# A hybrid decoder step: x turned before the launch, norms applied after the projections, decode selection first, and weight chunks of eight slices

## The chip, the cores and the metric

The kernel runs on one core of a Trainium2 chip. Its engines run side by side, each on its own queue in a fixed order: TensorE (PE: matmuls, transposes), VectorE (DVE), ScalarE (ACT), GpSimd (POOL) and SyncE (SP, which issues the DMA transfers here). The metric is the device time of one execution in microseconds. Three executions of the kernel before took 2206.09, 2209.12 and 2209.97 us; the median is 2209.12.

## The reference

One layer over 1024 prompt tokens and 32 decode tokens (8 sequences of 4), model width 2048. All inputs and weights are fp32.

```
xn = rmsnorm(x, norm_in)                       # mean square over 2048, times norm_in
p  = xn @ w_in    # q 8x128, k 2x128, v 2x128, z_attn 1024, q_idx 16x64, k_idx 64, w_idx 16,
                  # h, b, c, z_conv 1024 each
q, k, k_idx: rmsnorm over a head, then rotary on a quarter
I[t,s] = sum_h w_idx[t,h] * relu(q_idx[t,h] . k_idx[s])     # admissible s <= t
idx = top_k(I, 256)                            # prompt: of 1024; decode: of 8192 cached + own
attn = softmax(q . k[idx]) @ v[idx]            # decode gathers the selected rows from paged caches
conv, new_buf = width-3 causal convolution of c * h
mix = concat[attn * silu(z_attn), b * conv * silu(z_conv)]
y = x + mix @ w_out;   also returned: k, v, k_idx per token, conv buffers
```

## The kernel before

The tokens are worked in two blocks. Block 0 is prompt tokens 0 to 511 and the 32 decode tokens, 544 columns in two PSUM halves: 288 (prompt 256 to 511 and decode) and 256. Block 1 is prompt tokens 512 to 1023, 512 columns. In each block the same stages follow: index queries (`qi_tiles`, 8 tiles of 128 weight columns; in block 0 on the half of 288 alone), index keys (`ki_tile`, 80 weight columns), heads (`head_tiles`: 2 k, 2 v, 8 q), 8 gates (`z_tile`), and 8 convolution tiles (`conv_tiles`: c, h, b, z_conv). In block 0 the order is index queries, then index keys; in block 1 keys, then queries. Then come the output projections (`out_proj0` for block 0, `out_proj1` for block 1).

Every projection (`proj`) is exact to fp32 in three products: x and w are split into a rounded part and a remainder (xh, xl; wh, wl), and xh*wh, xl*wh and xh*wl are summed over 16 slices of 128 along the model width (L512). `load_w` loads a chunk of four such slices (tile w, 4 buffers), ScalarE casts it to wh and VectorE subtracts for wl (3 buffers each). A matmul of a slice so needs a chunk's wh and wl and the slice's xh and xl.

x comes in rows of tokens. `prep_x0` loads the rows of block 0, takes their norms (`x_rstd`), scales the rows, and then transposes them on TensorE (psx) slice by slice; `x_part` writes xh (ScalarE) and xl (VectorE) from PSUM, times norm_in. Block 1: `x_rms1` takes the norms on the side, `x1_load` loads the rows (xq), `x1_scale` scales them by rx1, and `prep_x1` transposes them between the matmuls of the last convolution tile of block 0 (`conv_tiles(0, 7)`).

The rest is side work in four pipes that are advanced at every `slot()` between chunks: main (scores of the index, attention), dec (decode attention), rms, and vec (the selections). A prompt selection (`prompt_select`) searches a threshold for the scores of 128 tokens; a prompt attention (`prompt_attend`) makes probabilities P, transposes them (pt) and multiplies with v. The decode selection (`decode_find`) compacts the selected positions of 32 tokens in a tile S of 128x2304 int16 in several rounds (L1226 to L1237: each round has two tensor_scalar and three tensor_tensor instructions on VectorE), takes the maximum over ways (`way`, L1239), and makes row numbers (`pg`, `nb`, `pt`, `ids`, `pidx`, `rid`) for the gathers. "dsel" is its end, and the heads of block 1 wait for it.

What order the engines' queues get is settled before the launch by the framework's list scheduler, which follows the program order and priorities (`first()` raises one); on the chip each engine takes its queue strictly in that order. VectorE's helper instructions all carry the line L121.

Of the kernel before, what the change touches and what calls it, by code (L numbers as in the profile page):

```python
# [8 lines left out]
F32 = mybir.dt.float32  # L9
# [104 lines left out]
def build(tc, ctx, I, O, stop=None):  # L114
# [80 lines left out]
    def w_in(ch, c0, m):  # L195

        if c0 == C_KI:
            return I["w_ki"][:, 4 * ch:4 * ch + 4]
        return I["w_in"][c0 // 128 if c0 < C_KI else 28 + (c0 - C_H) // 128, :, 4 * ch:4 * ch + 4]

    def w_out0(ch, c0, m):
        return I["w_out0"][c0 // 128, :, 4 * ch:4 * ch + 4]

    x_src = [(0, 128, xpr[256:384]), (256, 32, xsa), (128, 128, xpr[384:512]),
             (288, 128, xpr[0:128]), (416, 128, xpr[128:256])]
    x_raw = []

    def x_load(j):

        c0, n, src = x_src[j]  # L210
        if j == 0:
            big = gp.tile([128, 2304], F32, tag="sc", bufs=1, name="xsc")
            nc.sync.dma_start(big[:, 0:D], src)
            x_raw.append((c0, n, [(1024 * h, 1024, big[:, 1024 * h:1024 * h + 1024]) for h in range(2)]))
            return
        elif j < 4:
            parts = [(1024 * h, 1024, g4(name="xs")) for h in range(2)]
        else:
            parts = [(512 * h, 512, g2(name="xs2")) for h in range(4)]
        for a, w, t in parts:  # L220
            nc.sync.dma_start(t[:n, :w], src[:, a:a + w])
        x_raw.append((c0, n, parts))

    ident = const((128, 128), "ident")
    rows = e2((128, 256), name="rows")
    x_load(0)
    x_load(1)
    x_load(2)
    nc.vector.memset(rows, 0.0)
    nc.sync.dma_start(ident, I["cst"][:, 0:128])  # L230
    nc.sync.dma_start(rows[0:16, 0:128], I["norm_in"].rearrange("o (c p) -> (o c) p", p=128))
    nc.sync.dma_start(rows[32:56, 0:128], I["w_conv"].rearrange("o j (c p) -> (o j c) p", p=128))
    nc.sync.dma_start(rows[:, 128:256], I["state_conv"].rearrange("o s j (c p) -> (o s j c) p", p=128))
# [42 lines left out]
    w_d = dp.tile([512], F32, name="w_d", tag="w_d")  # L276

# [57 lines left out]
    rx1 = const((128, 4), "rx1")  # L335

    def x_part(k, ps, xs, hi, lo, a, w):

        for c0, n, parts in xs:
            if a <= c0 < a + w:  # L340
                for a2, w2, t in parts:
                    if a2 <= 128 * k < a2 + w2:
# [7 lines left out]
    def x_rstd(js, eng="av"):  # L350

        n = len(js)
        ss = sm((128, 2, n, 2), name="ssx")
        nc.vector.memset(ss, 0.0)
        for c, j in enumerate(js):
            _, rows_, parts = x_raw[j]
            for h, (a, w, t) in enumerate(parts):
                sqx = e2((128, 1024), BF, name="sqx")
                o = ss[:rows_, h % 2, c, h // 2:h // 2 + 1]
                if eng[h % 2] == "a":  # L360
                    nc.scalar.activation(out=sqx[:rows_, :w], in_=t[:rows_, :w], func=AF.Square, accum_out=o)
                else:
                    nc.vector.tensor_tensor_reduce(out=sqx[:rows_, :w], in0=t[:rows_, :w], in1=t[:rows_, :w], scale=1.0,
                                                   scalar=0.0, op0=MUL, op1=ADD, accum_out=o)
        v = sm((128, n), name="vx")
        tt(ss[:, 0], ss[:, 0], ss[:, 1], ADD)
        tt(v, ss[:, 0, :, 0], ss[:, 0, :, 1], ADD)
        ts(v, v, 1.0 / D, EPS, MUL, ADD)
        return rsqrt(v, n, "rx")

    def x_scale(j, h, r, c, eng=None):
        _, n, parts = x_raw[j]
        a, w, t = parts[h]
        if eng is nc.scalar:
            nc.scalar.activation(out=t[:n, :w], in_=t[:n, :w], func=AF.Copy, scale=r[:n, c:c + 1])
        else:
            (eng.tensor_scalar if eng else ts)(t[:n, :w], t[:n, :w], r[:n, c:c + 1], None, MUL)

    def prep_x0():

        x = x_tiles()

        def second():
            yield 1
            yield 1
            x_load(3)
            x_load(4)
            yield 1
            yield 1
            r = x_rstd((3, 4))  # L390
            for _ in range(4):
                yield 1
            for c, j in enumerate((3, 4)):
                for h in range(len(x_raw[j][2])):
                    x_scale(j, h, r, c)
            for _ in range(2):
                yield 1
            for k in range(KT):
                x_part(k, pj(name="psx"), x_raw, *x[k], 288, 256)
                yield 1  # L400
            hp[0] = 200
# [1217 lines left out]
```

## Time and profile before

| | |
|---|---|
| median of three runs | 2209.12 us |
| profiled execution | 2209.53 us, of which the span is 2207.6 us |
| TensorE | 2162.5 us busy, 98% of the span |
| VectorE, ScalarE, GpSimd | 1317.3, 1088.3 and 480.5 us |
| mean granted TensorE clock | 0.995 |
| DMA | 290.81 MB, mean 132 GB/s |

TensorE is busy nearly all the time, so a reader looks for the places where it is not, and for what ended each wait. The page's granted clock is 1.00 for 2.4 GHz; 0.50 is 1.2 GHz.

### The profile page before, as it was taken

The page shows a single profiled execution, that of the slowest core. Times are in us where ns is not written, and L with a number is a line of the kernel's source. Part 1 is how long each engine was busy: PE and PEld are TensorE (multiplying, and loading weights), DVE is VectorE, ACT ScalarE, POOL GpSimd, SP SyncE. Part 2 cuts the span into 40 slices and gives each one's busy share as a digit, 9 for nine tenths or more (in the row PEclk, how much of TensorE's full clock was granted, in tenths as well). Part 3 has the DMA queues.
Part 4 walks back from the last instruction along what each step waited for, and adds up shares of the span by engine and source line. Part 5 has one row for each costly group of instructions (what it writes and reads, how often), then busy time and mean ns, then how long its engine had stood idle before and what let it go on. Part 6 is the DMA issues. An engine that isn't in the chain of part 4 may idle for free.

```text
span 2207.6 us, 37829 instructions
## 1 busy us (share of the span) xinstructions
PE 2162.5 (98%) x13502; PEld 1941.8 (88%) x13502; DVE 1317.3 (60%) x2994; ACT 1088.3 (49%) x2112; POOL 480.5 (22%) x697
## 2 busy tenths in 40 slices
PE   6999999999999999999899999999999999999999
PEld 5899999999999999787688888888888899999887
DVE  6556666555555654799866666556667556443222
ACT  4346666334436566422257684445675565332221
POOL 2111011111113222142531143432331111210000
PEclk9999999999999999999999999999999999999999
DMA  5423444344344333333343344433343384448343
GB/s 195 131 90 117 125 138 135 118 141 131 123 144 140 118 116 104 107 117 113 102 134 117 117 150 129 118 122 105 113 128 113 102 301 117 123 119 275 134 134 110
DMA packets 203720, 290.81 MB, mean 132 GB/s; under 512 B 37588, under 2 KB 87948, under 8 KB 203404
## 3 DMA queue, kind: packets, MB, share of 16 engines
q1 hardware_dynamic: 192268, 254.83, 36.0%
q0 software_dynamic: 11264, 33.57, 5.5%
q8 instruction: 106, 1.74, 0.3%
q14 instruction: 82, 0.67, 0.1%
HBM read 247.53 MB, written 40.78 MB: 131 GB/s over the span
## 4 chain that ended last, share of the span: by engine, by line
PE 50%; DMA 0%; DVE 0%; issue 0%; POOL 0%
PE pj L512 33%; PE po L1503 8%; PE ix L855 1%; PE ix L854 1%; PE pt L174 1%; PE lg L1346 1%; PE dpo L1412 1%; PE kst L174 1%; PE sc L178 1%; PE sc L179 1%; PE po L179 1%; PE po L177 1%; PE po L178 1%; PE sc L177 1%; PE p L174 0%; PE pq L174 0%
## 5 line engine op out<-in xcount | busy, mean ns | idle before, releaser
L512 PE MATMUL pj<-xh,wl 128*128 128x288 f32 (+2 forms) x2800 | 793.0, 329 | 6.9 <-DVE wl L121 6.8
L512 PE MATMUL pj<-xh,wh 128*128 128x288 f32 (+2 forms) x2800 | 791.1, 328 | 6.9 <-DVE xl L121 2.7
L512 PE MATMUL pj<-xl,wh 128*128 128x288 f32 (+2 forms) x2800 | 796.1, 330 | 0.0
L121 DVE TENSOR_TENSOR wl<-w,wh 128x512 fp32r<-128x512 f32 (+1 forms) x613 | 444.1, 726 | 431.2 <-ACT wh L494 397.2
L494 ACT CAST wh<-w 128x512 fp32r<-128x512 f32 x616 | 379.2, 616 | 604.8 <-PE pj L512 380.0
L512 PEld LDWEIGHTS pj<-xh,wh 128*128 128x128 f32 (+1 forms) x2800 | 477.1, 189 | 51.8 <-DVE xl L121 3.1
L512 PEld LDWEIGHTS pj<-xh,wl 128*128 128x128 f32 (+1 forms) x2800 | 474.6, 189 | 51.6 <-DVE wl L121 11.2
L512 PEld LDWEIGHTS pj<-xl,wh 128*128 128x128 f32 (+1 forms) x2800 | 475.1, 189 | 42.2
L886 ACT ACTIVATE junk<-acc,se,se 128x512 int8<-128x512 f32 (+5 forms) x186 | 181.1, 974 | 27.4 <-DVE se L121 24.2
L1096 POOL DMA_INDIRECT G<-in_cache_kidx,gidx x64 | 64.3, 1004 | 388.6 <-PE gd L179 140.4
L121 DVE SCALAR_TENSOR_TENSOR acc<-ixr,wsg,acc 128x512 f32<-128x512 f32 (+3 forms) x150 | 98.3, 668 | 45.9 <-ACT ixr L857 44.7
L857 ACT ACTIVATE ixr<-ix,wab 128x512 f32<-128x512 f32 (+3 forms) x160 | 95.3, 613 | 54.9 <-PE ix L855 53.6
L512 PE MATMUL pj<-mxh,wl 128*128 128x272 f32 x512 | 109.8, 292 | 0.0
L512 PE MATMUL pj<-mxl,wh 128*128 128x272 f32 x512 | 109.4, 291 | 0.0
L512 PE MATMUL pj<-mxh,wh 128*128 128x272 f32 x512 | 108.9, 291 | 0.0
L1392 POOL DMA_INDIRECT Vs<-in_cache_v,rid x64 | 66.4, 1038 | 123.8 <-DVE Vl L121 36.1
L1004 ACT CAST pthl<-pt 128x256 fp32r<-128x256 f32 x144 | 49.6, 371 | 80.6 <-PE pt L174 79.4
L121 DVE TENSOR_TENSOR pthl<-pt,pthl 128x256 fp32r<-128x256 f32 x144 | 57.2, 420 | 50.6 <-ACT pthl L1004 50.0
L512 PEld LDWEIGHTS pj<-mxh,wh 128*128 128x128 f32 x512 | 81.5, 189 | 0.7
L512 PEld LDWEIGHTS pj<-mxl,wh 128*128 128x128 f32 x512 | 81.6, 189 | 0.3
L512 PEld LDWEIGHTS pj<-mxh,wl 128*128 128x128 f32 x512 | 81.3, 189 | 0.4
L990 POOL TENSOR_SCALAR P<-P,l 128x128 f32<-128x128 f32 (+7 forms) x64 | 51.9, 811 | 133.5 <-DVE l L989 102.7
(430 smaller groups left out, 3233.7 us busy)
## 6 DMA issues: line engine op xcount, KB each, us to landing
w<-in_w_in SPq DMA_DIRECT2D x480, 256.0 KB
w<-in_w_out SPq DMA_DIRECT2D x128, 256.0 KB
q_d<-qt SPq DMA_DIRECT2D x72, 64.0 KB
xr<-in_x_a SPq DMA_DIRECT2D x16, 272.0 KB
out_y_a<-xr SPq DMA_DIRECT2D x16, 272.0 KB
xq<-in_x_prompt SPq DMA_DIRECT2D x8, 512.0 KB
xq<-in_x_prompt SPq DMA_DIRECT2D x16, 256.0 KB
q<-q_d SPq DMA_DIRECT2D x32, 128.0 KB
```

The lines of the kernel that those rows point to most:

```text
L121: i = f(*a, **k)
L174: nc.tensor.transpose(out, in_, ident[:p, :p])
L177: nc.tensor.matmul(out, lh, rh, start=start, stop=False)
L494: nc.scalar.copy(hi, w)
L512: nc.tensor.matmul(p[:m, :n], w[c][:, k % 4], x[k][b][:, a:a + n], start=(k == 0 and c == b), stop=(k == KT - 1 and c == 1))
L857: nc.scalar.activation(out=r[:, :w], in_=ps[:, :w], func=AF.Relu, scale=wab[:, g, h:h + 1])
L886: nc.scalar.activation(out=junk[:, :n], in_=S, func=AF.Sign, scale=sg, bias=cand, accum_out=s)
L990: nc.gpsimd.tensor_scalar(P[:, :n], P[:, :n], l, 0.5, MUL, MUL)
L1004: nc.scalar.copy(t[:, 0], ptv)
L1096: nc.gpsimd.indirect_dma_start(out=G, out_offset=None, in_=cki, in_offset=bass.IndirectOffsetOnAxis(ap=idx[:, 8 * s + g:8 * s + g + 1], ax ...
L1392: nc.gpsimd.indirect_dma_start(out=W[:, hf], out_offset=None, in_=cv, in_offset=bass.IndirectOffsetOnAxis(ap=rid[:, hf, q:q + 1], axis=0))
L1503: nc.tensor.matmul(ps[i], x[k_][b][:, 128 * i:128 * i + 128], w[c], start=(k_ == 0 and c == b), stop=(k_ == KT - 1 and c == 1))
```

## The change

x is turned on the host into slices of 128 model columns by tokens (x_a 128x16x544 for block 0, x_b 128x16x512 for block 1), and norm_in, w_conv and state_conv are turned too, so the transposes of x on TensorE go. In block 0 the slices are multiplied by norm_in, split and projected at once; the token norms (rx) are taken from the rows later, in `second()`, and applied after the projections: R is the norm as a row broadcast to all partitions, R2 its square, and `gate`, `conv_tiles`, `v_rest` and `ki_rest` multiply by them, while k, q and k_idx take the norm into their epsilon (ex). In block 1 the turned slices are multiplied by R1, the broadcast of rx1 that is written to memory (r1_d) and read back.

`load_w` takes chunks of eight slices, w with 3 buffers, wl and wh with 2; `proj` uses four where it does more between chunks (`before`, `after`) or runs several tiles. `conv_tiles(0, 7)` now runs two tiles at a time. The index work of decode and its selection stand first in the pipes main and vec. The decode queries are made ahead of the decode attention in a unit of their own. The scaling of P moves from GpSimd to ScalarE.

```diff
-    def x_part(k, ps, xs, hi, lo, a, w):
-        for c0, n, parts in xs:
-            ...
-                        transpose(ps[:, c0 - a:c0 - a + n], t[:n, 128 * k - a2:128 * k - a2 + 128], n)
-        nc.scalar.activation(out=hi[:, a:a + w], in_=ps[:, :w], func=AF.Copy, scale=norm[:, k:k + 1])
-        stt(lo[:, a:a + w], ps[:, :w], norm[:, k:k + 1], hi[:, a:a + w], MUL, SUB)
+    def x_part(k, raw, hi, lo, a, w):
+        nc.scalar.activation(out=hi[:, a:a + w], in_=raw, func=AF.Copy, scale=norm[:, k:k + 1])
+        stt(lo[:, a:a + w], raw, norm[:, k:k + 1], hi[:, a:a + w], MUL, SUB)
+    def x_load(half, k, n):
+        ...
+        nc.sync.dma_start(t, I["x_a"][:, k:k + n, cols])
     def prep_x0():
+        nc.sync.dma_start(norm, I["norm_in"])
+        for c in range(4):
+            if c < 3:
+                early.append(load_w(w_in(slice(4 * c, 4 * c + 4), C_QI)))
+            raw = []
+            for n in ((1, 1, 1, 1), (2, 2), (2, 2), (2, 2))[c]:
+                raw += x_load(0, 4 * c + len(raw), n)
+            for k in range(4):
+                put(0, 4 * c + k, raw[k])
     def x1_load(ch, xs):
-            nc.sync.dma_start(t, xpr[512 + 256 * p:768 + 256 * p, 512 * ch:512 * ch + 512].rearrange(...))
+            nc.sync.dma_start(t, I["x_b"][:, 4 * ch + 2 * p:4 * ch + 2 * p + 2])
     def x1_scale(parts):
-        for i, (_, _, ((_, _, t),)) in enumerate(parts):
-            ts(t, t, rx1[:, i:i + 1], None, MUL)
+        for t in parts:
+            tt(t, t, R1[0].unsqueeze(1).to_broadcast([128, 2, 512]), MUL)
     def load_w(view, eng=None):
-            w = wp.tile([128, 4, 128], F32, tag="w", bufs=4, name="w")
-            lo = wp.tile([128, 4, 128], F32R, tag="wl", bufs=3, name="wl")
-            hi = wp.tile([128, 4, 128], F32R, tag="wh", bufs=3, name="wh")
+            w = wp.tile([128, 8, 128], F32, tag="w", bufs=3, name="w")
+            lo = wp.tile([128, 8, 128], F32R, tag="wl", bufs=2, name="wl")
+            hi = wp.tile([128, 8, 128], F32R, tag="wh", bufs=2, name="wh")
     def proj(src, c0s, m, x, cols, after=None, before=None):
+        step = 4 if after or before or len(c0s) > 1 else 8
     def gate(b, ps, out):
+        if b == 0:
+            for p, c in nat(b, ps):
+                tt(out[:, c], p, R[:, c], MUL)
     def conv_tiles(b, j, x, after=None):
-        group = 1 if after is None or b == 0 else 2
+        group = 1 if after is None else 2
-                nc.scalar.copy(ce[:, c], p)
+                if b == 0:
+                    tt(ce[:, c], p, R2[:, c], MUL)
+            if b == 0:
+                tt(y, y, R, MUL)
     def prompt_attend(i):
-            nc.gpsimd.tensor_scalar(P[:, :n], P[:, :n], l, 0.5, MUL, MUL)
+            ts(l, l, 0.5, None, MUL)
+            nc.scalar.activation(out=P[:, :n], in_=P[:, :n], func=AF.Copy, scale=l)
-    main.add(prompt_index(2), prompt_index(3), decode_index())
+    main.add(decode_index(), prompt_index(2), prompt_index(3), decode_queries())
-    vec.add(prompt_select(2), prompt_select(3), decode_select())
+    vec.add(decode_select(), prompt_select(2), prompt_select(3))
+    R1.append(g2(name="R1"))
+    nc.sync.dma_start(R1[0], r1_d.rearrange("(o n) -> o n", o=1).to_broadcast([128, 512]))
     for ch in range(3):
         x1_load(ch, xs)
-    nc = _bacc.Bacc("TRN2", target_bir_lowering=False, num_devices=1)
+    nc = _bacc.Bacc("TRN2", target_bir_lowering=False, num_devices=1, dynamic_dma_scratch_size=2048)
```

What the change does to the queues is seen at three places. The first is VectorE where the last tile of block 0 is read: cm is the gate of the convolution, pj the PSUM tile of z_conv, xl the remainder of block 1's x. Before:

```order
L121 SCALAR_TENSOR_TENSOR cm<-cm,pj 128x288
L121 SCALAR_TENSOR_TENSOR cm<-cm,pj 128x256
L121 TENSOR_SCALAR se<-tot,se_7576 128x1
L121 SCALAR_TENSOR_TENSOR xl<-psx,norm,xh 128x512
L121 TENSOR_TENSOR cm<-cm,y 128x544
L121 TENSOR_TENSOR se_7577<-se,se_7577 128x1
L121 SCALAR_TENSOR_TENSOR xl<-psx,norm,xh 128x512 x2
```

After, the same reading of pj, and 102 rows below it the first xl:

```order
L121 TENSOR_TENSOR cm<-pj,R 128x288
L121 TENSOR_TENSOR cm<-pj,R 128x256
L121 TENSOR_SCALAR S<-S 128x2304
L121 TENSOR_TENSOR wl<-w,wh 128x8x80
L121 TENSOR_SCALAR nm<-mx 128x1
L121 TENSOR_TENSOR S<-S 128x2304
```

```order
L121 TENSOR_TENSOR xq_10028<-xq_10028,R_10022 128x1024
L121 TENSOR_TENSOR xq_10030<-xq_10030,R_10022 128x1024
L121 TENSOR_SCALAR pt_9913<-pg_9910,ptc 128x256
L121 TENSOR_TENSOR xq_10032<-xq_10032,R_10022 128x1024
L121 TENSOR_TENSOR xq_10034<-xq_10034,R_10022 128x1024
L121 TENSOR_TENSOR pthl<-pt,pthl 128x256
L121 SCALAR_TENSOR_TENSOR xl<-xq_10024,norm,xh 128x512 x2
```

Before, seven xl stand ahead of the reading of pj and one two rows behind it; after, the first xl stands behind the compaction steps S<-S and what else came between, and directly behind the multiplies of xq by R1 (named R here).

The second place is TensorE at the same point of the program, the last matmuls of block 0 (128x288 and 128x256) and what follows. Before, where psx are transposes of x:

```order
L512 MATMUL pj<-xh,wl 128x288
L512 MATMUL pj<-xh,wl 128x256
L174 MATMUL psx<-ident,xq_10545 128x128 x2
L174 MATMUL psx<-ident,xq_10547 128x128 x2
L174 MATMUL psx<-ident,xq_10549 128x128 x2
```

After, where pt, lg, po and sc belong to attention:

```order
L481 MATMUL pj<-xh,wl 128x288
L481 MATMUL pj<-xh,wl 128x256
L174 MATMUL pt<-ident,P 128x128
L1327 MATMUL lg<-kih_87,zk_6824 128x512
L174 MATMUL pt<-ident,P 128x128
L177 MATMUL po<-pthl,vh_85 128x256
```

and, at the end of that work, the first matmuls of block 1's index keys (80x512):

```order
L179 MATMUL po<-pthl,vl_86 128x256
L177 MATMUL po<-pthl,vh_85 128x256
L481 MATMUL pj<-xh,wh 80x512
L178 MATMUL po<-pthl,vh_85 128x256
L179 MATMUL po<-pthl,vl_86 128x256
L481 MATMUL pj<-xl,wh 80x512
L481 MATMUL pj<-xh,wl 80x512
```

The transposes are gone; between the two projections only attention and one decode matmul are left.

The third place is SyncE, where the slices of block 1's x are loaded (xq, xq4). Before, in the convolution tiles of block 0, x is loaded as rows and nothing else is read back:

```order
L493 DMA w<-in_w_in 128x512 x4
L465 DMA xq_10547<-in_x_prompt 128x2x512
L465 DMA xq_10549<-in_x_prompt 128x2x512
L493 DMA w<-in_w_in 128x512
L465 DMA xq_10551<-in_x_prompt 128x2x512
L443 DMA xq<-in_x_prompt 128x512
```

After, the sixth of its loads (xq4) and the read of R1:

```order
L431 DMA xq4_10034<-in_x_b 128x1024
L1017 DMA zt_9885<-z_d0_118 128x2x128
L1244 DMA iota_9915<-in_dcst 128x256
L1247 DMA ptci_9917<-in_page_table 32x1x16 x2
L1022 DMA mx0_4h_128<-zt_9885 128x128
L1022 DMA mx0_5h_130<-zt_9885 128x128
L1023 DMA mx0_4l_129<-zt_9885 128x128
L1023 DMA mx0_5l_131<-zt_9885 128x128
L1247 DMA ptci_9917<-in_page_table 32x1x16 x2
L1556 DMA R1_10022<-r1_d_186 128x512
```

R1 is read behind the sixth load of x and behind the transfers of attention (zt, mx) and of the decode selection (iota, ptci).

## Rows read from the trace of the kernel before

**Rows 1.** The page's list of engines: busy us, share of the span, instructions
```profile
PE 2162.5 (98%) x13502; PEld 1941.8 (88%) x13502; DVE 1317.3 (60%) x2994; ACT 1088.3 (49%) x2112; POOL 480.5 (22%) x697
```

**Rows 2.** Windows: stretch, its length, busy us (instructions) of PE, PEld, DVE, ACT, POOL, PEclk, DMA
```profile
34.00:70.00 36.00, 32.20 (x215) 30.11 (x215) 28.12 (x64) 15.90 (x33) 8.49 (x9) 0.91 0.40 127
100.00:800.00 700.00, 700.00 (x5350) 680.38 (x5349) 399.45 (x951) 364.24 (x735) 123.39 (x180) 1.00 0.41 127
930.00:1075.00 145.00, 139.33 (x630) 111.14 (x629) 141.27 (x225) 39.54 (x78) 61.54 (x54) 1.00 0.34 109
1075.00:1090.00 15.00, 8.26 (x29) 6.20 (x29) 12.53 (x41) 2.79 (x5) 4.12 (x8) 0.66 0.23 70
1090.00:1100.00 10.00, 9.05 (x52) 7.38 (x50) 4.04 (x9) 3.42 (x7) 8.13 (x12) 1.00 0.54 166
```

**Rows 3.** Timeline of TensorE, start: start, length, instruction, [idle before <-releaser]
```profile
21.65 0.61 PE L512 MATMUL pj<-xh,wh 128*128 128x288 f32 x1 [0.24 <-ACT xh L344]
...
27.00 0.44 PE L512 MATMUL pj<-xl,wh 128*128 128x288 f32 x1
27.24 0.44 PE L512 MATMUL pj<-xh,wl 128*128 128x288 f32 x1
...
33.16 0.29 PE L512 MATMUL pj<-xl,wh 128*128 128x288 f32 x1
33.29 0.29 PE L512 MATMUL pj<-xh,wl 128*128 128x288 f32 x1
...
96.39 0.36 PE L512 MATMUL pj<-xh,wh 128*80 128x288 f32 x1 [1.85 <-DVE xl L121]
```

**Rows 4.** Timeline of TensorE where block 0 ends and block 1 begins
```profile
895.04 0.42 PE L512 MATMUL pj<-xh,wl 128*128 128x288 f32 x2
895.29 1.03 PE L174 MATMUL psx<-ident,xq 128*128 128x128 f32 x8
...
906.86 0.39 PE L512 MATMUL pj<-xl,wh 128*80 128x512 f32 x1
```

**Rows 5.** VectorE's instructions by form, 930 to 1090 us: count, busy us, mean ns
```profile
L121 DVE TENSOR_TENSOR S<-S 128x2304 int16<-128x2304 int16 x16 | 25.4, 1589 | 0.0
L121 DVE TENSOR_SCALAR S<-S 128x2304 int16<-128x2304 int16 x16 | 15.8, 986 | 0.1
...
L1239 DVE TENSOR_REDUCE way<-S 128x256 f32<-128x2304 int16 x1 | 4.2, 4227 | 0.0
```

**Rows 6.** DMA of the first 40 us: GB/s in slices of 1 us
```profile
GB/s 0 115 156 418 389 283 221 291 385 384 397 262 342 168 42 52 165 273 383 420 404 408 406 407 411 375 163 2 8 16 231 14 0 0 0 18 223 31 6 12
```

**Rows 7.** VectorE's instructions by form, whole span; the last row is ScalarE's
```profile
L121 DVE TENSOR_TENSOR wl<-w,wh 128x512 fp32r<-128x512 f32 x605 | 439.8, 728 | 424.3 <-ACT wh L494 390.5 <-ACT rh L1113 9.5 <-PE pj L512 7.0
...
L121 DVE TENSOR_TENSOR cm<-cm,y 128x544 f32<-128x544 f32 x8 | 5.8, 723 | 0.2
L121 DVE TENSOR_TENSOR cm<-cm,y 128x512 f32<-128x512 f32 x8 | 5.5, 690 | 0.2
...
L494 ACT CAST wh<-w 128x512 fp32r<-128x512 f32 x608 | 375.6, 618 | 590.3 <-PE pj L512 368.2 <-PE po L1503 129.0 <-issue 65.7
```

**Rows 8.** Timeline of VectorE in the decode selection, from doff to rid
```profile
969.30 0.16 DVE L121 TENSOR_SCALAR doff<-tot 128x1 f32<-128x1 f32 x1
...
1004.35 2.44 DVE L121 TENSOR_TENSOR S<-S 128x2304 int16<-128x2304 int16 x1
...
1034.27 0.75 DVE L121 TENSOR_SCALAR S<-S 128x2304 int16<-128x2304 int16 x1
1034.93 0.18 DVE L546 TENSOR_TENSOR ro<-kit,cst 128x32 f32<-128x32 f32 x1
...
1035.95 1.34 DVE L121 TENSOR_TENSOR S<-S 128x2304 int16<-128x2304 int16 x1
...
1092.40 0.22 DVE L1265 CAST rid<-pidx 128x64 int32<-128x64 f32 x1
```

**Rows 9.** Timeline of GpSimd beside one of them
```profile
1003.89 1.68 POOL L625 TENSOR_TENSOR qit<-qit,qish 128x512 f32<-128x512 f32 x1
```

More of the change, by code (lines that the diff above doesn't have):

```diff
@@ L371, in x_scale @@
[L371 to L377, printed above, removed]
+    def x_load(half, k, n):
+        _, w, cols = x_half[half]
+        t = g4((128, n, w), name="xs") if n > 1 else g2((128, n, w), name="xs1")
+        nc.sync.dma_start(t, I["x_a"][:, k:k + n, cols])
+        return [t[:, i] for i in range(n)]
@@ L379, in prep_x0, with put @@
     def prep_x0():
         x = x_tiles()
+        def put(half, k, raw):
+            a, w, _ = x_half[half]
+            x_part(k, raw, *x[k], a, w)
         def second():
-            yield 1
[L385 to L395, printed above, removed]
@@ new lines, in second @@
+            for k in range(0, KT + 2, 2):
+                for _ in range(2):
+                    yield 1
+                if k < KT:
+                    raw += x_load(1, k, 2)
+                if k:
+                    for c in (k - 2, k - 1):
+                        put(1, c, raw[c])
+            nc.sync.dma_start(ident, I["cst"][:, 0:128])
+            nc.sync.dma_start(cst, I["cst"][:, 128:])
+            nc.sync.dma_start(gi_, I["g_kidx"].to_broadcast([128, 64]))
+            hp[0] = 200
@@ L652, in k_rest @@
         yield from head_tok(b, raw, t, sq, v)
-        ts(v, v, 1.0 / 128, EPS, MUL, ADD)
+        while b == 0 and "rx" not in done:
+            yield 1
+        mean(b, v, 128)
         r = rsqrt(v, nt, "kr")
@@ L1286, in decode_attend @@
         zv = [const((128, 2, 144), f"zv{j}", F32R) for j in range(2)]
-        def zeros(ps, start):
-            nc.tensor.matmul(ps, zk[0][:, 0, 0:128], kih[0][:, :ps.shape[1]], start=start, stop=not start)
+        sc["qd"] = qd, zk, zv
         def queries():
@@ L1314, in queries, with decode_attend, zeros @@
             yield 1
-            st["q"] = 1
+            done.add("qd")
+        yield queries()
+    def decode_attend():
+        while not {"dsel", "z0", "qd"} <= done:
+            yield waiting
+        nb, rid = sc["nb"], sc["rid"]
+        qd, zk, zv = sc["qd"]
+        ck = I["cache_k"].rearrange("o n p h d -> (o n p) (h d)")
+        cv = I["cache_v"].rearrange("o n p h d -> (o n p) (h d)")
+        st = {}
+        def zeros(ps, start):
+            nc.tensor.matmul(ps, zk[0][:, 0, 0:128], kih[0][:, :ps.shape[1]], start=start, stop=not start)
         def keys(q):
@@ L1324, in keys @@
             yield 1
-            while "q" not in st or st.get("k") == dec.turn:
+            while st.get("k") == dec.turn:
                 yield 1
@@ L1441, in values @@
                 done.add("datt")
-        yield queries()
         for grp in range(2):
```

195 lines of the change are left out of this document (90 added, 105 removed).

## The prediction

> **What bounds the kernel now.** I read the page's list of engines first: TensorE is busy 2162.5 of the 2207.6 us span [rows 1], so only about 45 us of its waits, its half-clock stretches and its own instructions can be won, and every other engine counts only where it makes TensorE wait. The windows say where that is [rows 2]: from 100 to 800 us TensorE never stops; 34 to 70 and 930 to 1100 us have holes and stretches of lower clock. The timeline then shows the ends of each hole. At the start the first projection matmul comes at 21.65 us, behind transposes of x; these matmuls of 288 columns are 0.24 us apart at 27 us and 0.13 us at 33 us, and the index key projection of block 0 starts at 96.39 us [rows 3]. Between the last matmul of block 0 (895.04) and the second of block 1 (906.86) lie 11.8 us, filled with transposes of x and waits [rows 4]. From 930 us on VectorE is the engine that is waited for: it is busy 141.3 of the 145 us to 1075, and the widest of its work are the int16 steps of the compaction of the decode selection, S<-S [rows 2, 5].
>
> **The start.** What goes: the wait for a whole row block of x, its norm, and the transposes. What comes: x arrives turned, raw, in slices of 128x288 (147 KB), and the norm is read and worked out while projections run. The first matmul needs one slice and one 256 KB chunk of weights, 0.4 MB; DMA had moved that at 3.3 us [rows 6]; the cast of w takes 0.62 us [rows 7], that of xh about as much, beside DMA's latency: about 5 us. All 16 slices and four chunks are 3.4 MB, moved at 12.4 us by the same row; 48 matmuls at the 0.24 us of the first stretch end at 16.5; I take 17 for the first tile. Seven more tiles are 7 x 48 x 0.133 = 44.7 us, to 61.7. VectorE has shuffles, the second half of x and the casts' remainders in one queue there; the stretch from 34 to 70 us of before lost 3.8 us of idle time and 2.9 of clock (a granted 0.91 over 32.2 busy us) [rows 2]; I take 5 of these 6.7 again. So the key projection starts at 67, not 96.4: **-29.4 us**. Bounds: 62 without a stall (-34), 72 (-24).
>
> **x of block 1.** The 64 transposes of x go; 36 of them lie inside the 11.8 us above, the other 28 at 0.13 us (8 took 1.03 us) [rows 4] are **-3.6 us**.
>
> **The change of blocks, the largest term.** VectorE runs its queue in the written order. In the changed order it must read the last tile of block 0 (cm<-pj,R), and behind that stand 104 more instructions up to the first xl of block 1, which the second matmul of block 1 needs; before, the xl stood beside and even ahead of the same cm. Three causes meet there: the decode selection, put first, is now at its compaction in this place (it was at 969 to 1092 us [rows 8]); prompt block 3's selection and block 2's attention stand there too; and the scaled x needs R1, whose DMA is queued on SyncE behind an x load that waits for a buffer that the selection of prompt block 3 frees. Nothing of block 1 can go ahead, since TensorE's queue is in order as well; its other work in there is 63 small matmuls, some 8 us. The 105 instructions, by durations of before: 19 compaction steps 24.9 us (eight 2304-wide tensor-tensor ones at 1.589, seven of one tensor at 0.986, four narrower at about 1.32) and the reduction of ways 4.2 [rows 5]; 37 one-column steps at the 0.16 of doff, 6.0 [rows 8]; by the row of 544 columns, 0.72, or their share of it [rows 7]: the rest of the conv tile and a weight remainder 4.0, page numbers (nb, pg, pt) 4.2, attention and search, 23 of 256 to 512 columns, 11.4; six multiplies of x by R1. No 128x1024 one of two fp32 operands is in the trace: by the slope from 512 to 544 columns (690 and 723 ns) [rows 7] it takes 1.22 us, by two of the 728 ns ones 1.46; I take 1.22, since the slope is of the same operation, and 7.3 in all; first xl 0.75. Sum 62.8. Consecutive ones overlap (the one at 1034.27 lasts 0.75, the next starts at 1034.93) [rows 8]: I take 0.05 us each, so 57.5. That this kind of sum holds, the same stage of before shows: from doff to rid 205 instructions sum to 131.7, less 10 is 121, and they took 123.1 (969.30 to 1092.40) [rows 8]. With 0.4 us for the last matmul the stretch is 58 us in place of 11.8: +46. Then xl comes at one per 1.0 us (the next 18 entries, 17.4 us) where TensorE takes 3 x 0.23 us a slice: +3 (0 to 6). TensorE's clock after a stop: a granted 0.66 over 8.3 busy us at 1075 to 1090 cost 2.8 us [rows 2], of which the shorter stop of before has part already: +1. **+50 us.** Lowest by rows: S at 1.34 and 0.75 (clean, as at 1035.95 and 1034.27) takes 3.6 off, 0.1 us of overlap each takes 10.5: 48.7, so +37; highest without any overlap and two-step multiplies, +61.
>
> S took 2.44 us at 1004.35 and 1.34 at 1035.95 [rows 8]; beside the first GpSimd ran a sum of its own, from 1003.89 to 1005.57 [rows 9], beside the second nothing. The Trainium skill (Advanced Engine Details and Errata, Mode Summary) says why that can be: VectorE's second port to SBUF is shared with GpSimd, and instructions of both block each other. The scaling of P leaves GpSimd with this change, so by the rule the steps would run nearer 1.34, and the sum would be 3.6 us lower; by the mean of the rows it stays. The trace agrees with the rule.
>
> **What the early decode gives back.** The holes up to 1100 us were the wait for this same compaction, and for what is queued with it: idle 5.7 + 6.7 + 0.9 = 13.3 us in the three windows, and the 2.8 us of clock [rows 2]. The selection now ends before block 1's heads, and the index projection of block 1 has VectorE nearly to itself: **-16 us** (-10 if the key and head work there still waits, -18).
>
> **Chunks of eight.** 605 casts of 512 columns become 108 and 250 of 1024, which frees VectorE and ScalarE; neither bounds TensorE outside the places above, so that is worth nothing by itself, and 200-odd fewer DMA issues neither. Against it: two buffers of wl and wh in place of three. A chunk of eight lasts TensorE 8 x 3 x 0.25 = 6 us (0.23 x 24 = 5.6 in block 1); cast and remainder take 2 x 0.62 + 1.22 = 2.5 after a buffer comes free [rows 7], which leaves 3.1 to 3.5 us for queues, where three chunks of four left about 4.3. **+2 us** (0 to 8). out_proj1 keeps chunks of four on the new buffers and holds the last two k of a group together: the last chunk's cast can begin only when its buffer is released, so 0.62 + 0.73 [rows 7] less the 0.7 us of three matmuls is exposed, and again at the next group's first: some 1.5 us for each of four groups, **+6** (0 to 10).
>
> The multiplies by R and R2 in block 0 (VectorE gains some 25 us of work, and is busy 399 of the 700 us from 100 to 800), P's scale on ScalarE, decode queries first, the smaller DMA scratch: nothing, hidden under matmuls that do not stop from 100 to 800 us; without cover the gate's 0.7 us per tile would be late, 8 x 0.7.
>
> **Sum.** -29.4 - 3.6 + 50 - 16 + 2 + 6 = +9. The profiled execution took 2209.53 us, so 2218.5; the runs' median is 0.4 lower, so 2218.
>
> **Rivals.** *A, faster: VectorE gets through the change of blocks much quicker than the rows.* The other terms are -41; the stretch breaks even at a chain of 48.5 us, and is faster beyond noise below 44. For it: 2.44 us at 1004.35 against 1.34 [rows 8], so the means hold slow ones, and sums overstate. Against: the lowest that rows allow is 48.7, and the same kind of sum came out 2 us too low. At 40 us: 2209.5 - 41 + 40.4 - 11.8 + 4 = 2201. *B, slower still: two buffers bind.* 250 chunks with 3.3 us of slack in queues that made TensorE lose 5.7 us from 930 to 1075 with 4.3 [rows 2]; if one in four loses 0.25 us, +15: 2233. Against: TensorE never stopped in 700 us with VectorE at 57%. *C, no change: the start gives 7 us more*, the key projection at 60, since the matmuls are 0.13 us apart earlier and no cast is late: 2211. For it 61.7 without stalls; against, VectorE's queue order there. *D, that x isn't early*: slices wait behind weights on SyncE and the first tile ends at 25; this is in the upper end.
>
> **Chances.** Forecast 0.52, alone 2206 to 2232 (the bounds of the block's change and of the start, not all at one end); A 0.23; B 0.15; C with D 0.10. A measurement here can tell 0.2%, 4.4 us, from no change. Faster: 0.19 of A and 0.04 of C; same: 0.07 of the forecast, 0.04 each of A and C; the rest slower: 0.23, 0.15, 0.62. The range that leaves out two in ten goes from 2192 (start -34, chain 48.7) to 2240 (B with the block's change at +55).
>
> **What would show it.** A hole of 45 to 60 us in TensorE between the last matmul of block 0 and block 1's second, released by VectorE's xl, with VectorE at over 90% in it; the first key projection of block 0 at 62 to 72 us; no hole when the heads of block 1 start; holes of about 1 us at out_proj1's group ends. Wrong it is if that stretch is under 45 us, if TensorE has many short waits on wl between 100 and 800 us, or if the first tile ends after 22 us.

## The result and the profile after

The changed kernel takes 2238.82 us (median of 4 runs) beside 2209.55 for the kernel before: a ratio of 1.0134, 95% interval 1.0121 to 1.0146. It is 29 us slower; the forecast was 9. The time lies in the stated range of 2192 to 2240 by 1 us only, and above the 2206 to 2232 that the forecast had alone. The execution with a profile took 2235.97 us. The page's list of engines, which answers to [rows 1]:

```profile
PE 2152.8 (96%) x13356; PEld 1930.6 (86%) x13356; DVE 1281.1 (57%) x2790; ACT 1086.7 (49%) x1894; POOL 458.3 (21%) x630
```

TensorE is busy 9.7 us less and the span is 26.6 us longer, so its waits grew by 36 us. The windows show where (columns as in [rows 2]); below them one window around the change of blocks:

```profile
0.00:70.00 70.00, 55.17 (x364) 52.01 (x365) 43.75 (x77) 32.79 (x53) 18.80 (x23) 0.98 0.80 272
70.00:130.00 60.00, 54.79 (x415) 54.02 (x414) 25.51 (x69) 26.93 (x48) 8.14 (x10) 0.94 0.50 147
130.00:790.00 660.00, 660.00 (x5040) 640.68 (x5039) 382.41 (x820) 343.29 (x585) 117.48 (x150) 1.00 0.39 125
790.00:960.00 170.00, 119.82 (x761) 105.93 (x760) 152.12 (x330) 66.53 (x140) 41.30 (x54) 0.81 0.27 79
960.00:1130.00 170.00, 168.90 (x837) 138.60 (x835) 91.41 (x193) 58.93 (x102) 80.50 (x98) 1.00 0.41 133
...
876.00:940.00 64.00, 21.42 (x72) 14.64 (x72) 57.20 (x114) 22.58 (x48) 19.04 (x26) 0.55 0.21 64
```

From 130 to 790 us TensorE never stops, as before. The heads of block 1 (960 to 1130), which held the holes of before, are full. Most of what is lost lies from 790 to 960, and most of that in 64 us around the change of blocks: TensorE busy 21.4 us of 64 at a granted 0.55, VectorE 57.2 (89%). TensorE's timeline there (with [rows 4]):

```profile
876.43 0.42 PE L481 MATMUL pj<-xh,wl 128*128 128x288 f32 x2
...
887.02 0.48 PE L174 MATMUL pt<-ident,P 128*128 128x128 f32 x1 [7.92 <-ACT P L993]
...
902.43 0.69 PE L177 MATMUL sc<-kth,qhl 128*128 128x384 f32 x1 [9.39 <-DVE qhl L121]
...
911.68 0.47 PE L174 MATMUL pt<-ident,P 128*128 128x128 f32 x1 [6.53 <-ACT P L993]
...
925.70 1.28 PE L174 MATMUL pt<-ident,P 128*128 128x128 f32 x4 [7.25 <-ACT P L993]
...
938.55 0.58 PE L178 MATMUL po<-pthl,vh 128*128 128x256 f32 x1 [5.75 <-DVE pthl L121]
938.93 0.42 PE L179 MATMUL po<-pthl,vl 128*128 128x256 f32 x1
939.29 0.71 PE L481 MATMUL pj<-xl,wh 128*80 128x512 f32 x1
```

The last matmul of block 0 and the second of block 1 stand 62.9 us apart, against 11.8. The waits between are named P, qhl and pthl, which are attention. For qhl and pthl the engine behind them is VectorE, where their steps stand in line with the compaction; P is written by ScalarE from steps of the same line, and an experiment below takes its scale off ScalarE and leaves the stop:

```profile
878.10 0.77 DVE L121 TENSOR_TENSOR cm<-pj,R 128x288 f32<-128x288 f32 x2
878.80 0.74 DVE L121 TENSOR_SCALAR S<-S 128x2304 int16<-128x2304 int16 x1
879.47 1.34 DVE L121 TENSOR_TENSOR wl<-w,wh 128x640 fp32r<-128x640 f32 x1
880.73 0.14 DVE L121 TENSOR_SCALAR nm<-mx 128x1 f32<-128x1 f32 x1
880.79 1.34 DVE L121 TENSOR_TENSOR S<-S 128x2304 int16<-128x2304 int16 x1
...
927.86 0.18 DVE L1250 CAST ptc<-ptci 128x16 f32<-128x16 int32 x1 [2.33 <-DMA ptci<-in_page_table]
...
930.06 5.04 DVE L121 TENSOR_TENSOR xq<-xq,R 128x1024 f32<-128x1024 f32 x4
935.02 0.81 DVE L121 TENSOR_SCALAR pt<-pg,ptc 128x256 int16<-128x256 int32 x1
935.76 2.40 DVE L121 TENSOR_TENSOR xq<-xq,R 128x1024 f32<-128x1024 f32 x2
938.08 0.41 DVE L121 TENSOR_TENSOR pthl<-pt,pthl 128x256 fp32r<-128x256 f32 x1
938.42 2.15 DVE L121 SCALAR_TENSOR_TENSOR xl<-xq,norm,xh 128x512 fp32r<-128x512 f32 x3
```

And SyncE, where the read of R1 (named R) stands behind the sixth load of x, which waits for a buffer that eq<-acc frees at 911.39 (acc holds the scores of prompt block 3):

```profile
911.42 0.33 SPq L431 DMA_DIRECT2D xq<-in_x_b  x1
...
915.29 0.33 SPq L1244 DMA_DIRECT2D iota<-in_dcst  x1
...
926.30 0.38 SPq L1556 DMA_DIRECT2D R<-r_d  x1
```

VectorE itself did not wait for R1: its multiplies at 930.06 follow without a pause. What R1's late read sets is their place in VectorE's queue.

Three smaller losses are new, at 111.68, 831.28 and 2068.69. On TensorE the start, the wait for the page table, the queries of prompt block 2's attention (pq; the decode queries, pqd, had gone through at 665.9 without a wait) and the output projection:

```profile
5.50 0.61 PE L481 MATMUL pj<-xh,wh 128*128 128x288 f32 x1 [5.50 <-ACT wh L461]
...
72.73 0.41 PE L481 MATMUL pj<-xh,wh 128*80 128x288 f32 x2
...
111.68 0.68 PE L1059 MATMUL pp<-pt,dc 8*128 8x64 f32 x2 [4.81 <-DVE pt L1057]
...
831.28 0.69 PE L174 MATMUL pq<-ident,q 128*128 128x128 f32 x2 [5.15 <-POOL q L520]
...
2068.69 0.80 PE L1514 MATMUL po<-wh,mxh 128*128 128x512 f32 x1 [4.32 <-ACT wh L461]
```

The wait at 111.68 is a transfer: VectorE's instruction before it waits for the page table, 512 numbers of 4 bytes, issued at 101.75:

```profile
111.44 0.18 DVE L1057 CAST pt<-pt8i 8x64 f32<-8x64 int32 x1 [8.13 <-DMA pt8i<-in_page_table]
```

### The profile page after: what moved, and what is told of

Read it like the earlier page. It is cut to its first block, busy times and chain, and to the rows that moved or that the text cites. A ratio compares the mean times of both kernels' runs of the same rounds, so it can differ in the third digit from the quotient of the medians.

```text
span 2234.2 us, 36133 instructions
## 1 busy us (share of the span) xinstructions
PE 2152.8 (96%) x13356; PEld 1930.6 (86%) x13356; DVE 1281.1 (57%) x2790; ACT 1086.7 (49%) x1894; POOL 458.3 (21%) x630
## 4 chain that ended last, share of the span: by engine, by line
PE 89%; DVE 3%; DMA 3%; issue 2%; POOL 2%; ACT 1%; SPq 1%; DVEq 0%; POOLq 0%; ACTq 0%
PE pj L481 65%; PE po L1514 7%; PE ix L856 1%; PE ix L857 1%; PE pt L174 1%; PE gt L174 1%; PE sc L178 1%; PE sc L179 1%; PE sc L177 1%; PE dpo L1424 1%; PE po L179 1%; PE da L1122 1%; PE po L178 1%; PE gd L179 1%; PE po L177 1%
## 5 line engine op out<-in xcount | busy, mean ns | idle before, releaser
L121 DVE TENSOR_TENSOR wl<-w,wh 128x1024 fp32r<-128x1024 f32 (+2 forms) x362 | 398.6, 1102 | 328.1 <-ACT wh L461 201.1
L461 ACT CAST wh<-w 128x1024 fp32r<-128x1024 f32 (+2 forms) x362 | 331.5, 916 | 416.5 <-PE pj L481 225.9
L888 ACT ACTIVATE junk<-acc,se,se 128x384 int8<-128x384 f32 (+5 forms) x186 | 180.9, 973 | 41.1 <-DVE se L121 36.9
L960 POOL TENSOR_TENSOR q<-q,ssq 128x256 f32<-128x256 f32 x32 | 22.4, 698 | 474.8 <-DMA q<-q_d 426.5
L121 DVE TENSOR_TENSOR pthl<-pt,pthl 128x256 fp32r<-128x256 f32 x144 | 57.2, 419 | 82.6 <-ACT pthl L1007 82.5
L1020 POOL TENSOR_TENSOR zt<-zt 128x256 fp32r<-128x256 f32 x32 | 29.5, 921 | 348.9 <-ACT zt L1019 322.8
L1116 ACT ACTIVATE rh<-gd 128x512 fp32r<-128x512 f32 x64 | 38.3, 598 | 117.7 <-PE gd L179 117.6
L121 DVE SCALAR_TENSOR_TENSOR rl<-gd,rh 128x512 fp32r<-128x512 f32 x64 | 44.1, 690 | 83.7 <-ACT rh L1116 83.4
```

The costliest lines, as they stand in the source:

```text
L121: i = f(*a, **k)
L461: nc.scalar.copy(hi, w)
L888: nc.scalar.activation(out=junk[:, :n], in_=S, func=AF.Sign, scale=sg, bias=cand, accum_out=s)
```

## The experiments

Below, "lost" is a window's length less TensorE's busy time times its granted clock, so that idle time and low clock stand in one number. Medians of the kernel before in these comparisons were 2208.4 to 2209.5 us.

**R1 in a buffer of its own.** Theory T1, the one of the prediction: R1's place behind a buffer that the selection frees makes the stop.

```diff
-    R1.append(g2(name="R1"))
+    R1.append(const((128, 512), "R1"))
```

> The changed kernel with one edit: R1, the broadcast norms of block 1, gets a buffer of its own instead of one of the ten shared ones. Theory T1 (the stop at the change of blocks comes from R1: its read waits 125 us on SyncE for a shared buffer, and all multiplies and remainders of x stand behind it): the stop of 62.6 us between the last matmul of block 0 and the second of block 1 falls below 10 us, VectorE writes xl before it reads the last tile of block 0, and the time is about 2239 - 53 - 5 of clock and pace = 2181 (2174 to 2192). Theory T2 (the compaction of the decode selection is in VectorE's way there whatever R1 does): the stop stays above 40 us and the time at 2225 to 2239.

2234.55 us, ratio 1.0117 [1.0100, 1.0134]. The long stop is gone: block 1's second matmul comes 0.5 us after the last of block 0, its first is at 885.24 in place of 932.08, and 21.2 us are lost from 790 to 960 us in place of 72.9. R1's read is issued at 812.16, ahead of the last three loads of x (863.90 to 872.37), so it was the buffer that R1 itself shared that put it behind the sixth load. T1 holds for the place; T2's stop of over 40 us is not there, though its time (2225 to 2239) came true, since the kernel won 4 us, at the edge of the noise, where T1 had 58. The same two windows, 790 to 960 and 960 to 1130, of this run:

```profile
790.00:960.00 170.00, 155.01 (x947) 137.15 (x946) 154.11 (x295) 69.51 (x135) 42.64 (x45) 0.96 0.35 107
960.00:1130.00 170.00, 149.64 (x699) 119.89 (x698) 94.51 (x237) 60.15 (x114) 74.80 (x109) 0.92 0.37 112
```

From 960 to 1130 it loses 32.3 us where the changed kernel lost 1.1. TensorE's waits there are attention again, with no projection between its steps:

```profile
1043.78 0.33 PE L174 MATMUL pt<-ident,P 128*128 128x128 f32 x1 [3.52 <-ACT P L993]
...
1055.19 1.09 PE L174 MATMUL pt<-ident,P 128*128 128x128 f32 x2 [2.76 <-ACT P L993]
```

And the wait for R1 itself is not nothing: it is written at 803.24, its read is issued at 812.16, and VectorE waits for it:

```profile
817.71 3.50 DVE L121 TENSOR_TENSOR xq<-xq,R 128x1024 f32<-128x1024 f32 x3 [8.79 <-DMA R<-r_d]
```

**The prompt selections first again, in the changed kernel.**

```diff
-    main.add(decode_index(), prompt_index(2), prompt_index(3), decode_queries())
+    main.add(prompt_index(2), prompt_index(3), decode_index(), decode_queries())
-    vec.add(decode_select(), prompt_select(2), prompt_select(3))
+    vec.add(prompt_select(2), prompt_select(3), decode_select())
```

> The changed kernel with the order of the side work as before (prompt selections and index work 2 and 3 first, decode after; decode queries stay a unit of their own). 33 instead of 104 instructions stand on VectorE between the last tile of block 0 and the first xl, 16 us by durations of before: both theories expect the stop to fall from 62.6 to about 20 us, and the hole before the heads of block 1 (16 us of waits and clock) to come back. 2239 - 42 - 3 of clock + 16 - 7 (the early wait for the page table at 111 us) = 2203 (2196 to 2212). T1 alone expects that this stop is still ended by the read of R1 or the multiplies of x; T2 that nothing of it is R1's.

2242.01 us, 1.0149 [1.0132, 1.0166]. The stop falls to 21.6 us (870.85 to 892.42), as expected, and its last 5.0 us are a wait for xl behind the multiplies by R1, as T1 alone had it. So the 63 us needed both, R1's place and the decode work first. But as much comes back elsewhere: 40.0 us are lost from 960 to 1130 (18.3 in the kernel before) and 21.8 from 2000 to 2090, of which 9.0 are one wait for the attention's results (mxh). By the total, the order of decode and prompt is not why the changed kernel is slow.

**Decode first alone, in the kernel before** (the same two lines, the other way).

> The kernel before with one part of the change: decode index work and decode selection first. There is no R1 in it (x is scaled by a number per row). T1: no long stop at the change of blocks, since the remainders xl stand beside the last tile; some 15 us instead of 11.8; the hole at 1075 to 1090 us goes (-10 to -16); a wait for the page table may come early (+5): 2203 (2194 to 2210). T2: the compaction stops TensorE there as in the changed kernel: 2209 + 30 to 45 = 2240 to 2255.

2192.71 us, 0.9921 [0.9904, 0.9938]: faster than both. The stretch at the change of blocks is 16.4 us (885.20 to 901.58; T1 had 15), so T2 fell. The loss from 960 to 1130 falls from 18.3 us to 6.9, that of the first 70 us from 24.0 to 19.0. This part of the change is worth 16.6 us by itself, and not only at block 1's heads: the key projection comes 7.3 us earlier (89.09).

**Chunks of four again, in the changed kernel.**

```diff
-            w = wp.tile([128, 8, 128], F32, tag="w", bufs=3, name="w")
+            w = wp.tile([128, 4, 128], F32, tag="w", bufs=4, name="w")
...
-        step = 4 if after or before or len(c0s) > 1 else 8
+        step = 4
```

> The changed kernel with chunks of four slices in 4, 3 and 3 buffers as before. Both theories: the stop stays (90 instructions instead of 104, 49 us by durations of before, so some 54 instead of 62.6), the waits for wl of up to 2.4 us in the first 50 us and the 4.3 us wait in the output projection go or shrink: 2239 - 8 - 8 = 2223 (2214 to 2236). If it is above 2239, the larger chunks themselves paid.

2223.96 us, 1.0073 [1.0056, 1.0090], as expected to 1 us: 15 us of the 29 are the chunks' (the prediction had 8). The stop stays but is 9 us shorter, 54.0 us (63.2 us lost from 790 to 960); the wait in the output projection goes (8.0 us lost from 2000 to 2090 become 0.3). The start does not gain: the key projection comes at 73.36 (72.73).

**x turned alone** (chunks of four and the order of before).

> The changed kernel with the side work in the order of before and with chunks of four slices in 4, 3 and 3 buffers: what is left is x turned, norms later, R1 and P's scale on ScalarE. Theory T4 (chunks of eight cost what the run with chunks of four gained, 15 us, whatever else is changed): 2242 - 15 = 2227 (2221 to 2233). Theory T5 (they cost only together with the decode work first): 2242 (2237 to 2246). If x turned alone pays on the chip, as the 24 us earlier key projection suggests, it is below 2205; that is not expected, since this kernel still reads R1 late.

2236.18 us, 1.0129 [1.0109, 1.0148]: what is left (x turned, norms later, R1, P's scale on ScalarE, the decode queries as a unit of their own, the smaller DMA scratch) costs 28 us without the other two parts, with 35.2 us lost from 960 to 1130 and 22.8 from 2000 to 2090. T4 fell: in this company the larger chunks cost 6 us, which is at the edge of the noise. T5's range is missed by 1 us.

**P scaled on GpSimd again.** The waits in the stop are named P, so ScalarE is a suspect (T6).

> The changed kernel with the scale of P back on GpSimd. Theory T6 (the attention of prompt blocks 2 and 3 is late because ScalarE, busy 35 to 42 of 50 us from 550 to 750 us, takes P's scale in its queue behind the search steps): the attention is further when block 0 ends, the stop there falls by 5 to 15 us, 2226 to 2234. Rival (ScalarE's queue is not the chain that ends last): the stop stays within 4 us of 62.6, 2236 to 2242.

2240.99 us, 1.0146 [1.0129, 1.0163]: no gain. The stop is 60.2 us (882.23 to 942.43), and its waits only change their name (18.7 us for P from GpSimd, by the waits of TensorE over the whole span). T6 fell, the rival's numbers hold.

**R1's own buffer and chunks of four together.**

> The changed kernel with two edits that were run singly: R1 in a buffer of its own (2234.6) and chunks of four (2224.0). If each keeps its own worth (4 and 15 us, the stop only moving to the heads of block 1): 2220 (2214 to 2226). If the larger chunks were what brought the stop back at the heads of block 1 and at the output projection once R1 was out of the way: 2224 - 50 = 2175 (2168 to 2190).

2210.33 us, 1.0005 [0.9995, 1.0014]: as fast as before. Together they give 28 us where they gave 4 and 15 alone, so the parts do not add up, and neither expectation (2220, 2175) was met. Against the run with R1's buffer alone, 10.2 us less are lost from 960 to 1130 and 12.8 less from 2000 to 2090, where that run had waited 8.5 us for the attention's results; why the larger chunks delay that attention is not shown. TensorE's losses are still 21.1 us from 790 to 960 and 22.1 from 960 to 1130.

**R1 made on TensorE** (four transposes in place of the way through memory, into a buffer of its own), with chunks of four, the page table loaded at the start and P on GpSimd.

```diff
-                nc.sync.dma_start(r1_d.rearrange("(g p) -> p g", p=128), rx1)
+                nc.vector.tensor_copy(rb, rx1.unsqueeze(2).to_broadcast([128, 4, 128]))
+                for g in range(4):
+                    transpose(pr1[:, 128 * g:128 * g + 128], rb[:, g])
+                nc.scalar.copy(R1[0], pr1)
```

> The changed kernel with four edits: chunks of four; R1 made by four transposes of the broadcast norms instead of a write to memory and a read (9 and 5.5 us in the trace of the run with R1's own buffer, where VectorE stood for 8.8 us); the page table of the decode index loaded first of all (its transfer took 9.4 us and TensorE waited 4.8 for it at 111 us); P's scale on GpSimd. If nothing comes back elsewhere: 2192.7 (decode first alone) - 24 of the start - 3 = 2166 (2160 to 2180). If stops come back at the heads of block 1 as with R1's own buffer: 2205 to 2220.

2216.86 us, 1.0028 [1.0014, 1.0041]. The change of blocks is nearly clean (7.6 us lost), but 58.7 us are lost between 130 and 790, where no other run loses 6. From about 700 us up to the transposes at 748.03, which wait 10.3 us for rb, TensorE's queue holds no projection at all, only attention and search, with waits between their steps. A miss that shows how much a bad place in a fixed queue costs.

**Only block 0's x turned** (block 1 as before the change, by transposes; chunks of four; decode first), **then the page table loaded at the very start, then P on GpSimd.**

> The changed kernel with block 1's x as before (rows, scaled by a number per row, transposed on TensorE, no R1; the last convolution tile of block 0 in single tiles again) and chunks of four. Theory T1 in its wider form (the loss is all in how block 1's x is prepared: R1 is a chain of two transfers that stands in VectorE's and SyncE's queues): the remainders stand beside the last tile again, the stop is about 15 us, and the 24 us of the early start are kept: 2192.7 - 24 + 8 (the wait for the page table at 111 us and its clock) = 2177 (2168 to 2187). Theory T8 (an earlier start only brings block 0 to its end sooner, while the side work, which ends last, doesn't get done sooner, so TensorE waits as long somewhere else): 2192 to 2210.

> The same with the page table of the decode index loaded at the very start. T1: the wait of 5 to 9 us at 111 us and its clock go, nothing comes back: 8 us under the run without it, 2169 (2160 to 2180). T8: no change against the run without it, within 4 us.

> The same once more with P's scale back on GpSimd. If ScalarE's queue held the attention up where no other stop covers it: 5 to 10 us under the run with P on ScalarE. If not: within 4 us of it, as in the run where this edit alone was made.

2205.88 us, 0.9982 [0.9973, 0.9992]; 2201.35 us, 0.9962 [0.9948, 0.9976]; 2201.55 us, 0.9974 [0.9964, 0.9985]. The first lies in T8's range and 19 us above T1's upper bound. The early page table removes the wait on pp, 9.1 us here, and gives at most 4.5 us (the intervals overlap, and the two profiled executions, 2201.64 and 2202.71, show no gain), since another wait of 5.1 us stands in its place at 117.92. P on GpSimd changes nothing here either. All three start block 0's keys 15 us or more earlier than decode first alone, and end later. When block 1's first matmul and the first weight load of its output projection come, in us:

| kernel | block 1 starts | output projection | between |
|---|---|---|---|
| before | 906.6 | 2026.5 | 1120 |
| decode first alone | 901.4 | 2012.0 | 1111 |
| only block 0 turned | 892.4 | 2016.9 | 1125 |
| R1 buffer, chunks of four | 889.2 | 2025.9 | 1137 |
| R1 buffer | 885.2 | 2032.8 | 1148 |
| changed kernel | 932.1 | 2042.8 | 1111 |

In all runs with decode first up to here, block 1 takes 1100 to 1114 us when it starts at 901 or later, and 1125 to 1148 when it starts earlier; with decode last it takes 1120 from a start at 907 and 1134 to 1138 from one at 883 to 887. What an early start wins is lost again, as T8 says. The proposed reason is that the work on the side (decode selection, attention of prompt blocks 2 and 3) then still stands in block 1's first 200 us, one step waiting for the other; the last run tests it.

**Attention of prompt block 3 later**, on the run with the page table first.

```diff
-    main.add(*(prompt_attend(i) for i in range(4)))
+    main.add(*(prompt_attend(i) for i in range(3)))
...
-    main.add(prompt_index(4), prompt_index(5), prompt_attend(4), ...
+    main.add(prompt_index(4), prompt_attend(3), prompt_index(5), prompt_attend(4), ...
```

> This is the run with block 0 turned and the page table first, with the attention of prompt block 3 moved from the queue of block 0's side work to block 1's, behind the index of prompt block 4. T8: when block 1 starts early, its first 200 us are slowed because attention of prompt blocks 2 and 3 and the decode selection are still to be done there, with TensorE waiting on P (3.1 us at 1053) and on pthl; put off by half of that work, the waits on P and pthl between 1040 and 1070 us go and the idle time of 960 to 1130 us falls from 9.9 to under 5: 2201.35 becomes 2192 to 2197, and the first output projection comes 4 to 9 us earlier. Rival T9: those waits are only where the holes show, and the heads of block 1 wait for the end of the decode selection whatever stands beside it; the holes move to other work at the same place and the time stays within 3 us of 2201.

2183.44 us, 0.9877 [0.9859, 0.9894], the fastest of all: 18 us less than without the move, more than T8 had said. The window of 960 to 1130 us, first without the move:

```profile
960.00:1130.00 170.00, 160.08 (x783) 129.78 (x782) 100.45 (x240) 65.54 (x132) 71.11 (x106) 0.97 0.42 124
```

and with it:

```profile
960.00:1130.00 170.00, 169.26 (x854) 138.67 (x853) 107.31 (x232) 73.26 (x144) 70.85 (x94) 1.00 0.44 134
```

Idle time falls from 9.9 to 0.7 us and the clock is full: 14.0 us of the 18. T9, that the holes would move to other work, fell. P's transposes show the move: per 50 us from 900 on they were 6, 10, 20 and 8 instructions, and are 6, 6, 0 and 0, with the rest beside projections after 1100. The first weight load of the output projection comes at 1998.3 in place of 2018.7: block 1, started at 891.9, takes 1106 us.

## Why the prediction was right, and where its sizes failed

**Direction and place were right.** It named the change of blocks as the largest term, and the hole, VectorE's part in it and R1's place on SyncE are all in the trace. That the time lies inside the range is partly luck: the sum was 17.6 us too low, and the range reached 2240 only by rival B. The four stretches it summed, by the span: to block 0's keys, then to its last matmul, then to block 1's second, then to the end. Of the +50 for the change of blocks 46 are the stretch itself; the 4 for pace and clock lie behind block 1's second matmul and stand in the last row.

| stretch | forecast | measured |
|---|---|---|
| to the key projection | -29.4 | -23.7 |
| to block 0's last matmul | -3.6 | +5.1 |
| the change of blocks | +46 | +51.0 |
| the rest (+4 -16 +2 +6) | -4 | -5.8 |
| sum | +9 | +26.6 |

**The change of blocks** was put at 58 us and took 62.9; that +50 and +51.0 look alike is luck. VectorE's chain took 60.3 us from cm to the start of the first xl, and 61.0 to its end, where 57.5 were summed, and it was made up otherwise: the compaction ran at 1.34 and 0.75 us, the clean durations, not the means of [rows 5], so that VectorE was busy 4 us less than summed, while it waited 6.7 us inside the chain for ScalarE and a transfer, which the sum left out. The multiply of 128x1024 took 1.20 to 1.26 us (1.22 forecast).

The clean durations don't come from P's scale leaving GpSimd, as the prediction had it. With P back on GpSimd the 24 tensor-tensor steps on S still have a median of 1.35 us and at most 1.75; and in the kernel before, S at 1000.44 took 1.33 us beside the scale of P, which began at 1000.69 and took 1.65 us where its form takes 1.00 on the mean. In the changed kernel GpSimd works beside some of the steps too, and it is GpSimd that slows down. A step of 128x32 takes 1.37 us beside the S of 880.79, which keeps its 1.34, and 0.25 us at 911.47 where no S runs:

```profile
880.88 1.37 POOL L516 TENSOR_TENSOR ro<-q,cst 128x32 f32<-128x32 f32 x1
...
911.47 0.25 POOL L516 TENSOR_TENSOR ro<-q,cst 128x32 f32<-128x32 f32 x1
```

In these pairs the one that began first kept its time: S here, and GpSimd in [rows 9], whose 1.68 us stand beside a mean of 1.59 for its form.

**The start: the step that failed is the 5 us given for stalls.** The first matmul came at 5.50 as said, the first tile was read at 21.80 (22 was the bound), the key projection came at 72.73, just past the upper bound of 72. TensorE stood idle for 14.8 us in the first 70, 9.3 of them behind the first matmul, and lost 1.1 more by the clock, with waits on xh, wh and wl up to 2.4 us. The widest ones are VectorE's order: the remainder of a chunk stands behind the reading of a tile that TensorE has still to finish. Before 43.31 VectorE had waited 4.75 us for such a tile, and TensorE then waited for the remainder that followed:

```profile
43.31 0.01 DVE L602 LOAD_MASK_SELECT qish<-pj  x1 [4.75 <-PE pj L481]
...
44.05 1.69 DVE L121 TENSOR_TENSOR wl<-w,wh 128x1024 fp32r<-128x1024 f32 x1
...
45.79 0.40 PE L481 MATMUL pj<-xh,wl 128*128 128x288 f32 x1 [2.26 <-DVE wl L121]
```

**"Nothing, hidden under matmuls that do not stop" is the step that cost most.** Of the 17.6 us that the sum is off, 8.7 are in that stretch. It counted what the edits add, and not what they move: with decode put first its page table is needed at 111 us, 9.7 us after its load is issued. TensorE waited 4.8 us and then ran 8 us, from 112 to 120, at a granted 0.63 (3.0 us more); and the attention of prompt block 2, which the new order puts behind the decode work (its first scores come at 836.37, 804.07 before), made it wait 5.2 us for its queries from GpSimd at 831.28. These feed TensorE itself, so the matmuls around them were no cover. What the wait for the page table costs in the end is less sure: where the table was loaded early, 9.1 us of it went and at most 4.5 us were won. From 130 to 790 us the cover held: TensorE never stopped.

**The chunks' terms had the wrong mechanism.** The sum gave them 8 us, the run with chunks of four 15: 9 in the stop, whose queue is longer by 14 instructions, and 8 in the output projection, less 3 at the page table, where the wait is 7.9 us with chunks of four. The group ends of the output projection, given 6 us, cost nothing: in both kernels the groups end 44.20 us apart. What was late is the first group's weights, 4.3 us at 2068.69. And the experiments give chunks of eight 15 us here, 6 (at the edge of the noise) with the old order and 24 with R1's own buffer; a single number for such a part does not exist in this kernel.

**What the early decode gives back** held in its place: the loss from 960 to 1130 falls from 18.3 us to 1.1 in the changed kernel, where -16 was said. That the run with decode first alone also won 16.6 us is a coincidence, since 7.3 of these lie at the start. By the total it gives the changed kernel 3 (2242.01 against 2238.82), which is not clear of the noise, since the stop takes its place.

**The rivals.** A (VectorE's chain much quicker) fell, 60.3 us against 48.5. B came nearest in time, 2233, but not in mechanism: its many short waits between 100 and 800 us are not there, from 130 to 790 us two buffers never bind. C fell at 72.73, D with the first tile read at 21.80, not 25. Two signs of the forecast missed narrowly (the stop was to be 45 to 60 us, with VectorE busy for over 90% of it), and the holes at the group ends were not there.

**What stays open.** The cause named for the stop is shown, but not as the cause of the 29 us: without it 25 remain, in other holes, and only with chunks of four as well are the 29 gone. Then the 24 us of the earlier start should show as a gain, and they don't: block 1 takes 1137 us there in place of 1120. Between the run with R1's own buffer and the changed kernel, 11 to 12 us of the difference lie neither in idle time nor in the clock. That the side work's place eats the early start is shown by the last run, for a kernel that turns only block 0's x; with both blocks turned the same move was not run. Nor was it run on the kernel with decode first alone, so it is open how much of the 18 us it would give without an early start; that kernel loses 6.9 us in the window where 14.0 of the 18 were won.

## What to carry to other kernels

Where one engine is 98% busy, an edit is priced by what it moves in the other queues, and the price of a part depends on which other parts stand beside it: time each part alone and together, since here one part was worth -16.6 us alone and -3, within the noise, in company. When a stage starts earlier, look at what side work now falls into it without cover, and move that work too: one such move was worth 18 us here. A wait that is removed at one place should be followed through the rest of the span before it is counted as won: here most of a removed stop came back at the next stage and in the output projection, over 1000 us later.

## What the runs showed of the hardware

Two transfers of 512 numbers of 4 bytes were slow for 2 KB: in the changed kernel the page table took 9.7 us from issue to its reader, and in the run with R1's own buffer 8.9 us passed from the issue of R1's write to that of its read, with 5.5 more until the reader of that began. TensorE's granted clock was 0.55 on average over the 64 us at the change of blocks, in which it was busy for a third of the time, and 0.63 over 8 busy us after a pause of 4.8. Steps of VectorE and GpSimd that ran side by side cost each other time: a GpSimd step of 128x32 took 1.37 us in place of 0.25, and an S of 128x2304 in the kernel before 2.44 in place of 1.34.
